# Following a short TensorE matmul with a long one from another thread, and new step times in the scheduler's recorded clock

## The chip, the core and the metric

The kernel runs on one core of a Trainium2 chip. The metric is the device time of one execution, in microseconds (us). The profile names the engines PE (TensorE matmuls), PEld (TensorE weight loads), DVE (VectorE), ACT (ScalarE), POOL (GpSimd) and SP (SyncE, which starts the transfers).

## The reference

Two layers of a diffusion backbone work on 256 context tokens and 512 latent tokens of width 1024. Cut to what matters:

```
u = rms_norm(h) * (1 + scale) + shift                 # scale, shift, gate = silu(c) @ w_ada
rq, rk, rv, rg, gq, gk, gv, gg, glr, ma, mb = split(u @ w_in)
ret = chunked retention of rq, rk, rv, both directions, 4 heads
gla = chunked gated linear attention of gq, gk, gv, decay from glr, both directions, 4 heads
y_ret = (group_norm(ret) * silu(rg)) @ w_branch_ret
y_gla = (head_rms_norm(gla) * silu(gg)) @ w_branch_gla
h = h + gate * ((sigmoid(ma) * y_ret + sigmoid(mb) * y_gla) @ w_out)
```

After the second layer the latent stream gets a last rms_norm. The second layer needs no outputs for the context tokens.

## The kernel before, in words

Every large product is made as three products of rounded parts (`mm3`: high by high, high by low, low by high), accumulated in PSUM. A matmul instruction has a 128x128 stationary operand, loaded by its own weight load, and a moving operand whose columns decide its length: 512 for projections over the latent tokens or over a weight block (into `pj` tiles), 256 for projections over the context, for the states (`xp`), for the outputs of a head (`op`) and for the branch projections that read the normalised heads `z`, and 128 for score products and for transposes (`tr`, line 319, into `xp`). The program holds 10,136 matmul instructions: 3,104 of 512 columns, 192 of 384, 5,968 of 256, 848 of 128 and 24 of 2. Below, "short" means under 256 columns and "long" the others.

The order on every engine comes from a scheduler that runs while the kernel is built (class `Emit`). Work is written as threads, generators that record instructions. They are ranked: evacuations of PSUM, weights, scans (the heads' transposes, scores, states, outputs), low, and main (the projections). The scheduler holds a recorded clock for each engine. `run` goes through the threads in rank; an instruction for another engine than PE is issued once it is ready on the recorded clock, and of the PE instructions that are ready, the first in rank is issued. The recorded clocks settle only the order: the chip waits on semaphores, so a wrong estimate makes an engine wait, or puts work later than need be.

The cost of a matmul on the recorded clock is set in `mm` and `tr`, and the clock is moved on in `issue`:

```
c = (max(n, 256) if r.dtype == F32R else max(4 * n, 512)) / 2400 + 0.0023
...
self.op("pe", 0.11, (i,), (o,), lambda: self.nc.tensor.transpose(o, i, ident))
```

That is 0.216 us for 512 columns, 0.109 us for 256 and for 128, and 0.11 us for a transpose.

Of the kernel before, what the change touches and what calls it, by code (L numbers as in the profile page):

```python
# [13 lines left out]
F32R = mybir.dt.float32r  # L14
# [29 lines left out]
def _pieces():  # L44
    """Name of every 4 KiB-per-partition weight piece of a layer, in the order of use."""
    names = []
    for h in range(H):
        names += [("rqkv", h, i) for i in range(4)] + [("rg", h, j) for j in range(2)]
    for oc in range(KC):
        names += [("ma", oc), ("wr", oc)]  # L50
    names.append(("glr",))
    for h in range(H):
        names += [("gk", h), ("gq", h)] + [("gv", h, i) for i in range(2)] + [("gg", h, j) for j in range(2)]
    for oc in range(KC):
        names += [("mb", oc), ("wg", oc)]
    names += [("wo", oc) for oc in range(KC)]
    return {n: i for i, n in enumerate(names)}
# [125 lines left out]
def view(ap, off, dims):  # L183
    """A free-form view of a tile: its partitions, and [step, count] pairs from element off on."""
    return bass.AP(tensor=ap.tensor, offset=ap.offset + off, ap=[list(ap.ap[0])] + [list(d) for d in dims])
# [11 lines left out]
EVAC, WEIGHTS, SCAN, LOW, MAIN = range(5)  # L197

# [20 lines left out]
class Emit:  # L219
    """Puts the program into order. The work is written as threads: generators that record instructions and name, at  # L220
    each yield, what they need to go on. Whenever an engine is about to run dry, the first thread in rank whose next
    instruction there has its operands is let through. The clocks are estimates that settle nothing but this order."""

    def __init__(self, nc, sb, ps, dr):
        self.nc, self.sb, self.ps, self.dr = nc, sb, ps, dr
        self.uid = 0
        self.clk = {"pe": 0.0, "act": 0.0, "dve": 0.0, "pool": 0.0, "sp": 0.0, "dma": 0.0}
        self.end = {}
        self.table = None
        self.free_n = dict(SLOTS)  # L230
        self.slot = {k: [0.0] * n for k, n in SLOTS.items()}
        self.threads = []
        self.cur = None
        self.subs = []
        self.began = set()
        self.read = {}
        self.tick, self.cols, self.warm = 0, 0, False

    # tiles
# [45 lines left out]
    # instructions  # L285
# [3 lines left out]
    @staticmethod  # L289
    def keys(aps):  # L290
        """What instructions wait on: tiles, or the token groups of a stream tile."""
        r = []
        for a in aps:
            if isinstance(a, bass.AP):
                nm = a.tensor.name
                if nm.startswith("stream"):
                    t = a.offset % T
                    r += [(nm, g) for g in range(t // 256, (t + a.shape[-1] - 1) // 256 + 1)]
                else:
                    r.append(nm)  # L300
        return tuple(r)
# [5 lines left out]
    def mm(self, o, l, r, start, stop):  # L307
        n = self.n(r)
        c = (max(n, 256) if r.dtype == F32R else max(4 * n, 512)) / 2400 + 0.0023
        self.op("pe", c, (l, r), (o,), lambda: self.nc.tensor.matmul(o, l, r, start=start, stop=stop))  # L310
        self.cur.queue[-1].cols = n if r.dtype == F32R else 4 * n
# [6 lines left out]
    def tr(self, o, i, ident):  # L318
        self.op("pe", 0.11, (i,), (o,), lambda: self.nc.tensor.transpose(o, i, ident))  # L319
# [41 lines left out]
    def split_to(self, x, tag="g"):  # L361
        """The parts of x in new tiles: (hi, lo)."""
        shape = x.shape[1:]
        h, l = self.get(tag, shape, F32R), self.get(tag, shape, F32R)
        self.split(h[0], l[0], x)
        return h, l
# [8 lines left out]
    # order  # L375
# [7 lines left out]
    def after(self, gen, prio=SCAN, heavy=False):  # L383
        """Spawns a thread when all that its maker has recorded is out."""
        self.pseudo(lambda: self.spawn(gen, prio, heavy))

    def fill(self, th):
        """Lets a thread record its next step, if it has all it asked for."""
# [5 lines left out]
        for tag in SLOTS:  # L394
            n = w.get(tag, 0)
# [15 lines left out]
    def issue(self, th, op, ready):  # L411
        th.queue.pop(0)
        e = op.eng
        t = max(self.clk[e], ready)
# [5 lines left out]
        else:  # L420
# [4 lines left out]
            if e == "pe":  # L425
                c *= self.pace(t, op.cols)
# [11 lines left out]
    def lag(a, b):  # L438
        """From the end of one engine's instruction to the start of another's that waits for it."""
# [4 lines left out]
    def pace(self, t, cols):  # L444
        """TensorE's clock rests in a tick after one with few columns."""
# [7 lines left out]
    def run(self):  # L453
        while self.threads:
            now = self.clk["pe"]
            soon, moved, first = None, False, None
            for th in list(self.threads):
# [27 lines left out]
                if ok <= now and e == "pe":  # L485
                    first = first or (th, op, ready)
                elif ok <= now:
# [5 lines left out]
            if not moved and first:  # L493
                self.issue(*first)
# [5 lines left out]
class Weights:  # L500
    """The weight pieces in the order of their use, loaded and split ahead of it."""
# [44 lines left out]
class Block:  # L546
    """A weight block of 8 chunks of the contraction, n columns wide, taken half a piece at a time."""
# [24 lines left out]
def body(ctx, tc, io, out):  # L572
# [11 lines left out]
    # ---- constants  # L584
# [20 lines left out]
    # ---- the order of the projections, and with it that of the weights  # L605
# [30 lines left out]
    # ---- norm over the model width  # L636
    class Norm:
# [5 lines left out]
        def add(self, g, kp, h):  # L643
            """A step of a thread: h holds two chunks of a group's stream [128, 2, 256]."""
# [61 lines left out]
    # ---- conditioning  # L706
# [17 lines left out]
    def load_c():  # L724
        """silu(c) of both streams along the free axis, on all partitions: four tiles (vector, half)."""
# [16 lines left out]
    def ada_dve(cr, junk, raw, acc):  # L742
        """acc [128, 2, 2] (vector, half) = the rows of a transposed piece times both conditioning vectors."""
# [14 lines left out]
    def ada_first(kp, C, A, ev, begun):  # L758
        """Conditioning of two chunks in the first layer: the shift on VectorE, the scale on TensorE."""
# [37 lines left out]
    def ada_late(todo, done, then=None):  # L797
        """Conditioning that is not needed yet, on VectorE."""
# [32 lines left out]
    # ---- pieces shared by the two branches  # L831
# [14 lines left out]
    def spawn_states(hd, full):  # L846
        """The two state recurrences of a head. hd.kd[g]: hi, lo [128 tok, dir, tile, dk]."""
# [38 lines left out]
    def out_tile(hd, o, i, t, ph, pl, qh, ql):  # L886
        """o [128 tok, dv] of one tile: the scores' part and what the states bring."""
# [12 lines left out]
    def gate_out(hd, on, gain, g):  # L900
        """Normalised heads [tok, 2, dv] times gain and gate, feature-major."""
# [46 lines left out]
    def feat(src, sp, evac, wait=None):  # L948
        """Feature-major products with a weight block; src(k, a, n) gives parts of [a, a + n) as (offset, hi, lo)."""
# [22 lines left out]
    # ---- retention  # L972
# [91 lines left out]
    def rproj_outer(l, hd, R, full, u_ev, begun):  # L1064
        """The first head's projection, chunk by chunk of the contraction as the chunks come."""
# [131 lines left out]
    # ---- gated linear attention  # L1197
# [48 lines left out]
    def gdec(hd, Z):  # L1246
        """hd.G[g] [channel, dir, token]: the decay logs summed within each 128 tokens (times 16)."""
# [172 lines left out]
    # ---- merge  # L1420
    def gate_pair(B, pair, full, late):
        """The merge gates of two output chunks."""
# [80 lines left out]
    def out_unit(l, gs, hold, norm, m_ev, read_ev, hk, hn):  # L1503
        """The output projection of some groups, the gated residual, and the squares for the next norm."""
# [28 lines left out]
    def last(kp, g, h, norm):  # L1533
        """The final norm's gain and the output."""
# [5 lines left out]
    # ---- the whole  # L1540
# [137 lines left out]
```

## Time and profile before

| | |
|---|---|
| time, median of 3 runs | 1609.39 us (1609.18 to 1609.75) |
| span of the profiled execution (the page gives no other time of it) | 1609.0 us |
| PE busy | 1582.4 us (98%) |
| PEld busy | 1438.7 us (89%) |
| DVE busy | 1110.1 us (69%) |
| ACT busy | 837.7 us (52%) |

The span runs from the first to the last instruction of the one profiled execution. Busy time of PE overlaps: a matmul's recorded duration is longer than the distance to the next one's start, so the distance between starts is what counts. Chains of waits, rows of the timeline and waits by engine are in the section of rows.

### The profile page before, as it was taken

How to read it: one execution, taken by the hardware profiler on the slowest of the kernel's cores; microseconds unless marked ns; L12 is line 12 of the kernel's file. 1: busy time of each engine (PE TensorE's matmuls, PEld its weight loads, DVE VectorE, ACT ScalarE, POOL GpSimd, SP SyncE). 2: the span in 40 equal slices, each digit the busy share in tenths (PEclk: the TensorE clock that was granted, in tenths of full speed). 3: DMA queues.
4: the chain of work that ended last, by engine and by line, in shares of the span. 5: the costliest groups of instructions: out<-in, count | busy, mean ns of one | idle time of the engine just before them, and what ended most of it. 6: DMA issues, size and time to landing. Idle time of an engine off the chain costs nothing.

```text
span 1609.0 us, 26505 instructions
## 1 busy us (share of the span) xinstructions
PE 1582.4 (98%) x10224; PEld 1438.7 (89%) x10224; DVE 1110.1 (69%) x2526; ACT 837.7 (52%) x1783; POOL 37.7 (2%) x52
## 2 busy tenths in 40 slices
PE   7999999999999999999999999999999999999997
PEld 4788888989998999998998988988899999898997
DVE  8877485617877868776396765776657778877465
ACT  6734143421267778666333653443424767857443
POOL 0000000000000000000000000000000000000000
PEclk9999999999999999999999999999999999999999
DMA  9312122216621112112356421321355211213452
GB/s 347 128 46 66 45 67 66 92 54 236 209 67 53 60 47 66 42 53 91 128 200 205 146 71 58 92 79 53 118 199 170 65 66 53 80 54 103 155 186 92
DMA packets 71182, 169.37 MB, mean 105 GB/s; under 512 B 7440, under 2 KB 15760, under 8 KB 71056
## 3 DMA queue, kind: packets, MB, share of 16 engines
q1 hardware_dynamic: 71056, 167.69, 31.6%
q8 instruction: 80, 1.31, 0.3%
q14 instruction: 46, 0.38, 0.1%
HBM read 151.93 MB, written 15.73 MB: 104 GB/s over the span
## 4 chain that ended last, share of the span: by engine, by line
PE 93%; DVE 2%; issue 2%; ACT 1%; DMA 1%; POOL 0%; SPq 0%; POOLq 0%; DVEq 0%; ACTq 0%
PE pj L310 78%; PE xp L310 8%; PE op L310 6%; PE xp L319 2%; ACT g L329 1%; DVE g L342 0%; DVE p L342 0%; DVE g L352 0%; POOL v L370 0%; ACT p L329 0%; DMA g<-in_xT 0%; DMA wraw<-in_w 0%; DVE wlo L342 0%; SPq L373 0%; ACT whi L329 0%
## 5 line engine op out<-in xcount | busy, mean ns | idle before, releaser
L310 PE MATMUL pj<-streamh,whi 128*128 128x512 f32 (+1 forms) x1280 | 441.9, 346 | 0.6 <-ACT g L329 0.6
L310 PE MATMUL pj<-streaml,whi 128*128 128x512 f32 (+1 forms) x1280 | 441.4, 345 | 0.6 <-DVE streaml L342 0.6
L310 PE MATMUL pj<-streamh,wlo 128*128 128x512 f32 (+1 forms) x1248 | 430.5, 345 | 0.0
L329 ACT ACTIVATE whi<-wraw 128x512 fp32r<-128x512 f32 x350 | 217.5, 629 | 271.9 <-PE pj L310 248.4
L342 DVE TENSOR_TENSOR wlo<-wraw,whi 128x512 fp32r<-128x512 f32 x350 | 236.7, 686 | 161.8 <-ACT whi L329 159.8
L310 PEld LDWEIGHTS pj<-streamh,whi 128*128 128x128 f32 x1280 | 242.8, 190 | 26.1 <-ACT g L329 1.0
L310 PEld LDWEIGHTS pj<-streaml,whi 128*128 128x128 f32 x1280 | 242.9, 190 | 24.3 <-DVE streaml L342 0.8
L329 ACT ACTIVATE g<-g 128x512 fp32r<-128x512 f32 (+2 forms) x428 | 227.9, 564 | 64.9 <-DVE g L352 30.4
L310 PEld LDWEIGHTS pj<-streamh,wlo 128*128 128x128 f32 x1248 | 236.6, 190 | 24.3
L310 PE MATMUL pj<-whi,streamh 128*128 128x256 f32 (+2 forms) x744 | 247.8, 333 | 0.8 <-ACT whi L329 0.6
L310 PE MATMUL pj<-wlo,streamh 128*128 128x256 f32 (+2 forms) x744 | 247.8, 333 | 0.3 <-DVE wlo L342 0.3
L310 PE MATMUL pj<-whi,streaml 128*128 128x256 f32 (+2 forms) x744 | 247.3, 332 | 0.3 <-DVE streaml L342 0.3
L329 ACT ACTIVATE g<-pj 128x256 f32<-128x256 f32 (+4 forms) x296 | 107.6, 397 | 241.7 <-PE pj L310 241.3
L310 PE MATMUL pj<-g,whi 128*128 128x256 f32 x1280 | 230.5, 283 | 0.0
L342 DVE TENSOR_TENSOR g<-g,g 128x512 fp32r<-128x512 f32 (+2 forms) x312 | 198.2, 649 | 32.1 <-ACT g L329 30.1
L310 PEld LDWEIGHTS pj<-g,whi 128*128 128x128 f32 x1280 | 199.9, 192 | 0.3
L310 PE MATMUL pj<-g,wlo 128*128 128x256 f32 x640 | 181.1, 283 | 0.0
L310 PE MATMUL xp<-g,g 128*128 128x256 f32 (+1 forms) x928 | 152.2, 277 | 2.1 <-DVE g L342 1.8
L310 PEld LDWEIGHTS pj<-whi,streamh 128*128 128x128 f32 x744 | 141.5, 190 | 12.7 <-ACT whi L329 0.7
L310 PEld LDWEIGHTS pj<-whi,streaml 128*128 128x128 f32 x744 | 141.6, 190 | 11.8 <-DVE streaml L342 0.7
L310 PEld LDWEIGHTS pj<-wlo,streamh 128*128 128x128 f32 x744 | 141.5, 190 | 11.9 <-DVE wlo L342 0.5
L342 DVE TENSOR_TENSOR g<-pj,g 128x128 f32<-128x128 f32 (+4 forms) x163 | 60.9, 410 | 128.3 <-ACT g L329 128.2
(99 smaller groups left out, 1832.7 us busy)
## 6 DMA issues: line engine op xcount, KB each, us to landing
wraw<-in_w SPq DMA_DIRECT2D x175, 512.0 KB, 3.6
g<-in_adat SPq DMA_DIRECT2D x80, 256.0 KB, 4.7
g<-in_w SPq DMA_DIRECT2D x38, 256.0 KB, 5.5
g<-in_xT SPq DMA_DIRECT2D x24, 256.0 KB, 5.2
z<-g SPq DMA_DIRECT2D x20, 256.0 KB, 2.0
g<-z SPq DMA_DIRECT2D x20, 256.0 KB, 4.2
m<-g SPq DMA_DIRECT2D x20, 256.0 KB, 3.4
g<-m SPq DMA_DIRECT2D x20, 256.0 KB, 4.8
```

Of the source, the lines that this page charges most:

```text
L310: self.op("pe", c, (l, r), (o,), lambda: self.nc.tensor.matmul(o, l, r, start=start, stop=stop))
L319: self.op("pe", 0.11, (i,), (o,), lambda: self.nc.tensor.transpose(o, i, ident))
L329: lambda: self.nc.scalar.activation(out=out, in_=in_, func=func, scale=scale, **kw), TABLE.get(func))
L342: lambda: self.nc.vector.tensor_tensor(out=out, in0=a, in1=b, op=op))
```

## The change

Two things change in the scheduler, and nothing in what is computed. First, `issue` remembers whether the last PE instruction was short. If it was, `run` issues the first ready PE instruction in rank that is long, where there is one, and not the first in rank. Second, the recorded clock gets other step times: 0.0133 us are added to the columns' time instead of 0.0023, a short one costs at least 0.06 us and no longer 0.109, and a weight load takes 0.108 us and may start when the matmul before it starts. Comments and docstrings also go, which moves line numbers by 3 to 8.

```diff
+STEP, LOAD, SHORT = 0.0133, 0.108, 0.06
...
+        self.mm_at = self.ld_at = -1.0
+        self.short = False
...
     def mm(self, o, l, r, start, stop):
         n = self.n(r)
-        c = (max(n, 256) if r.dtype == F32R else max(4 * n, 512)) / 2400 + 0.0023
+        c = max(n / 2400 + STEP, SHORT) if r.dtype == F32R else max(4 * n / 2400 + 0.005, 2 * LOAD)
...
     def tr(self, o, i, ident):
-        self.op("pe", 0.11, (i,), (o,), lambda: self.nc.tensor.transpose(o, i, ident))
+        self.op("pe", SHORT, (i,), (o,), lambda: self.nc.tensor.transpose(o, i, ident))
...
             if e == "pe":
+                ld = max(self.mm_at, self.ld_at + LOAD)
+                t = max(t, ld + SHORT)
+                self.mm_at, self.ld_at, self.short = t, ld, op.cols < 256
                 c *= self.pace(t, op.cols)
...
                 if ok <= now and e == "pe":
                     first = first or (th, op, ready)
+                    if op.cols >= 256:
+                        long = long or (th, op, ready)
...
             if not moved and first:
-                self.issue(*first)
+                self.issue(*(long if long and self.short else first))
```

The two places below are on PE. A row has the line, the instruction, the tile written, the tiles read and the output's size.

The first is in the second layer's retention, where four transposes of a head's queries and values come due (`cst` is the identity) beside state products (`xp<-g,g`) and a projection (`pj`). Before:

```order
L310 MATMUL xp_10928<-g_10709,g_10923 128x256
L310 MATMUL xp_10930<-g_10710,g_10922 128x256
L310 MATMUL xp_10930<-g_10709,g_10923 128x256
L319 MATMUL xp_10932<-cst,g_10805 128x128 x4
L310 MATMUL pj_10872<-whi_10680,streamh_84 128x512
L310 MATMUL xp_10943<-g_10709,g_10922 128x256
L310 MATMUL xp_10943<-g_10710,g_10922 128x256
```

With the change:

```order
L322 MATMUL xp_10932<-cst,g_10798 128x128
L313 MATMUL pj_10872<-whi_10678,streamh_84 128x512
L322 MATMUL xp_10932<-cst,g_10798 128x128
L313 MATMUL xp_10942<-g_10701,g_10922 128x256
L313 MATMUL xp_10942<-g_10702,g_10922 128x256
L313 MATMUL xp_10942<-g_10701,g_10923 128x256
L313 MATMUL xp_10949<-g_10701,g_10922 128x256
L313 MATMUL xp_10949<-g_10702,g_10922 128x256
L313 MATMUL xp_10949<-g_10701,g_10923 128x256
L322 MATMUL xp_10932<-cst,g_10798 128x128
L313 MATMUL pj_10872<-wlo_10679,streamh_84 128x512
L322 MATMUL xp_10932<-cst,g_10798 128x128
```

The four transposes stood in one run, and now each has long matmuls behind it. In the whole program the short ones stood in 196 runs, 38 of them of a single matmul and 78 of four; now they stand in 837 runs, 827 of them single. Of the singles 25 were followed by a matmul of 256 columns and 13 by one of 512 before; now 420 are followed by 256, 389 by 512 and 18 by 384. In 325 of the stretches between two shorts there is now exactly one matmul of 256 columns, and in 300 exactly one of 512.

The second place is at the end of the second layer's last gated head: its last four transposes, and the branch projection that reads the head's `z`. Before, the transposes were followed by 24 matmuls of 512 columns of the merge gates and then by the branch projection, of which the first rows with `z` of the last group (`g_17134` high, `g_17135` low) are shown:

```order
L310 MATMUL pj_17197<-g_16980,whi_16907 128x256
L310 MATMUL pj_17197<-g_16981,whi_16907 128x256
L310 MATMUL pj_17197<-g_16980,wlo_16908 128x256
L310 MATMUL pj_17197<-g_17134,whi_16907 128x256
L310 MATMUL pj_17197<-g_17135,whi_16907 128x256
L310 MATMUL pj_17197<-g_17134,wlo_16908 128x256
```

With the change (`xp_17211` are the transposes, `g_17213` and `g_17214` the high and low part of the `z` made of them):

```order
L322 MATMUL xp_17211<-cst,g_17201 128x128
L313 MATMUL pj_17154<-g_16386,whi_16889 128x256
L322 MATMUL xp_17211<-cst,g_17201 128x128
L313 MATMUL pj_17154<-g_16385,wlo_16890 128x256
L322 MATMUL xp_17211<-cst,g_17201 128x128
L313 MATMUL pj_17154<-g_16445,whi_16889 128x256
L313 MATMUL pj_17154<-g_16446,whi_16889 128x256
L313 MATMUL pj_17154<-g_16445,wlo_16890 128x256
L313 MATMUL pj_17154<-g_17013,whi_16889 128x256
L313 MATMUL pj_17154<-g_17014,whi_16889 128x256
L313 MATMUL pj_17154<-g_17013,wlo_16890 128x256
L313 MATMUL pj_17154<-g_17213,whi_16889 128x256
```

The first use of the last `z` stood 63 long matmuls behind the last transpose, and now stands six behind it.

## Rows read from the trace of the kernel before

**Rows 1.** The page: span, and the chain that ended last by engine.

```profile
span 1609.0 us, 26505 instructions
...
PE 93%; DVE 2%; issue 2%; ACT 1%; DMA 1%; POOL 0%; SPq 0%; POOLq 0%; DVEq 0%; ACTq 0%
```

**Rows 2.** Busy time by stretch: length, engines, granted clock, DMA share, GB/s.

```profile
0.00:35.00 35.00, 23.52 (x112) 16.07 (x113) 27.12 (x78) 20.52 (x38) 2.75 (x7) 0.90 0.98 344
35.00:495.00 460.00, 459.42 (x2857) 410.82 (x2856) 310.58 (x807) 187.04 (x400) 9.44 (x12) 1.00 0.31 101
495.00:735.00 240.00, 236.95 (x1660) 220.03 (x1659) 177.66 (x337) 182.24 (x406) 8.72 (x10) 1.00 0.16 52
...
925.00:930.00 5.00, 3.90 (x22) 3.13 (x20) 4.54 (x12) 3.61 (x6) 0.00 (x0) 0.99 0.62 200
...
1275.00:1500.00 225.00, 224.60 (x1462) 204.19 (x1461) 174.59 (x327) 163.08 (x364) 6.17 (x8) 1.00 0.22 71
```

**Rows 3.** Waits of PE: us in total, times, longest.

```profile
PE pj L310 <- DMA cst<-in_cst: 4.7, 1, 4.7
...
PE op L310 <- ACT g L329: 0.5, 1, 0.5
```

**Rows 4.** Timeline, PE: a single short between matmuls of 256 columns.

```profile
522.01 0.28 PE L310 MATMUL pj<-whi,streamh 128*128 128x256 f32 x1
...
524.05 0.22 PE L310 MATMUL xp<-g,g 128*128 128x128 f32 x1
524.11 0.34 PE L310 MATMUL pj<-whi,streaml 128*128 128x256 f32 x1
524.29 0.28 PE L310 MATMUL pj<-whi,streamh 128*128 128x256 f32 x1
...
524.52 0.28 PE L310 MATMUL pj<-whi,streaml 128*128 128x256 f32 x1
```

**Rows 5.** Timeline, PEld: the weight loads at the same place.

```profile
524.05 0.19 PEld L310 LDWEIGHTS pj<-whi,streaml 128*128 128x128 f32 x1
...
524.16 0.19 PEld L310 LDWEIGHTS pj<-whi,streamh 128*128 128x128 f32 x1
```

**Rows 6.** Timeline, PE: a single short between matmuls of 512 columns.

```profile
506.93 0.39 PE L310 MATMUL pj<-streamh,wlo 128*128 128x512 f32 x1
...
508.29 0.22 PE L310 MATMUL xp<-g 128*128 128x128 f32 x1
...
508.63 0.39 PE L310 MATMUL pj<-streamh,whi 128*128 128x512 f32 x1
...
509.10 0.33 PE L310 MATMUL xp<-g,g 128*128 128x128 f32 x2
```

**Rows 7.** Timeline, PE: a run of four shorts before matmuls of 512 columns.

```profile
1143.10 0.60 PE L319 MATMUL xp<-cst,g 128*128 128x128 f32 x4
...
1143.77 0.39 PE L310 MATMUL pj<-streamh,whi 128*128 128x512 f32 x1
...
1144.92 0.39 PE L310 MATMUL pj<-streamh,wlo 128*128 128x512 f32 x1
```

**Rows 8.** Timeline, PE: a run of four shorts before matmuls of 256 columns.

```profile
540.15 0.60 PE L319 MATMUL xp<-cst,g 128*128 128x128 f32 x4
540.50 0.48 PE L310 MATMUL op<-g,p 128*128 128x256 f32 x2
540.82 0.64 PE L310 MATMUL op<-g,g 128*128 128x256 f32 x4
```

**Rows 9.** Timeline of three engines: last transposes of the last gated head, to `z`.

```profile
1497.99 0.80 PE L319 MATMUL xp<-cst,g 128*128 128x128 f32 x4 [0.40 <-ACT g L329]
...
1498.83 0.48 DVE L352 SCALAR_TENSOR_TENSOR g<-xp,small,g 128x256 f32<-128x256 f32 x1 [1.95 <-PE xp L319]
...
1500.34 0.63 ACT L329 ACTIVATE g<-g 128x512 fp32r<-128x512 f32 x1 [0.98 <-DVE g L352]
...
1501.01 0.69 DVE L342 TENSOR_TENSOR g<-g,g 128x512 fp32r<-128x512 f32 x1 [0.70 <-ACT g L329]
```

More of the change, by code (lines that the diff above doesn't have):

```diff
@@ L455, in run @@
             now = self.clk["pe"]
-            soon, moved, first = None, False, None
+            soon, moved, first, long = None, False, None, None
             for th in list(self.threads):
```

## The prediction

> **What bounds the kernel now.** I read the page first: of a span of 1609.0 us the chain that ended last is TensorE's for 93% [rows 1]. [...] The first 35 us, with 11.5 us idle, wait for transfers and the first norm, and the diff changes nothing they consist of. The products of a head's outputs, which read the states, waited for ACT once, 0.5 us [rows 3]. So two sums decide: what the sequence of matmuls costs when nothing waits, and the few microseconds of waits.
>
> Next, what one matmul costs in that sequence: the timeline, read by the distance between starts, since recorded durations overlap. Seventeen matmuls of 256 columns start within 522.01 to 524.05, so 0.120 us each; six of 512 within 506.93 to 508.29, so 0.227 us each [rows 4, 6].
>
> **The change: its first part, a long matmul behind a short.** It pays if a short followed by a long costs less than one followed by a short. The price of a short is read as the time from its start to the start of the second matmul behind the run, less one long step.
>
> Run of four before 256: 540.15 to 540.82 holds four shorts and two longs (the row of x2), 0.67 - 2 x 0.120 = 0.43, or 0.108 each; the trace has 30 such runs [rows 8]. Run of four before 512: 1143.10 to 1143.77 is 0.67 - 0.227 = 0.443, or 0.111 each; 29 such runs [rows 7].
>
> Single between 256s: it starts at 524.05, the long behind it only 0.06 later, which looks like a bargain. But the next long starts at 524.29, 0.18 after the one before it and not 0.12. The short has cost 0.24 - 0.12 = 0.12; over the 24 places of this kind the median is 0.116 [rows 4]. Between 512s: 508.29 to 508.63 is 0.34 - 0.227 = 0.115 with the starts unrounded, the median of ten places [rows 6]. The reason stands in the load rows: the weight load for the matmul behind the short starts with the short, at 524.05, and the load after that at 524.16. A load holds its place for 0.11 us, the short has columns for about half of that, and the remainder is waited for, whoever comes next [rows 5]. The early start of the long is a recorded start; the time comes back in its own step.
>
> So a single is dearer than a member of a run. The order holds 789 more singles than before: 395 with 256 columns behind, 376 with 512, 18 with 384.
> - Behind 256: 0.116 - 0.109 (the median of the 30 runs) = 0.007, x 395 = 2.8 us. Bounds: at 524.29 to 524.52 two steps take 0.23 and not 0.24, so some of it comes back; at 0.003 it is 1.2 us, and at the rounded 0.12 - 0.112 it is 3.2.
> - Behind 512: 0.115 - 0.111 = 0.004, x 376 = 1.5 us. Bounds: the two steps behind the single take 508.63 to 509.10, 0.47 and not 0.454, so it may cost 0.131 in all, while the five steps behind the run of four take 1.15 and not 1.135, so a member costs 0.115: a difference of 0.016, 6.0 us at most; at least 0, if the after-effect does not repeat when shorts and longs alternate strictly, of which the trace has no stretch.
> - Behind 384: 18 x 0.006 = 0.1 us.
>
> Sum: **+4.4 us**, with bounds from +1.2 to +9.3.
>
> [...]
>
> **The second part, the recorded clock.** No instruction is added. For 512 columns the recorded step goes from 0.216 to 0.227, for 256 from 0.109 to 0.120, which are the steps of the trace [rows 4, 6]. A short went in at 0.109 or 0.11, near its real 0.11; now it moves the clock by 0.067, or 0.108 behind another short, so a single is some 0.02 to 0.05 too cheap. The recorded clock of longs ran 5 to 10% ahead of the chip and the slack this left goes. A chain of 1.6 us on DVE and ACT was covered by 1.6 / 0.109 = 14.7 matmuls of 256 columns, which take 1.76 us, and is now covered by 13.3, 1.60 us: 0.17 us less. Where more than that was to spare nothing is felt, and that the output products waited only 0.5 us in all says it mostly was [rows 3]. I set this at 0, with bounds: all 5.1 us of idle time behind 35 us gone, or 24 of the chains (four heads, two branches, three groups) late by 0.17 us, 4 us.
>
> **One place where the order itself makes a wait.** In the second layer's last gated head the last transposes now stand six matmuls ahead of the first use of their `z`, where 63 stood before. The chain was seen there before [rows 9]: the row of four transposes ends at 1498.79, and with the 0.22 or more that one lasts [rows 4] the last starts at about 1498.5; DVE's first product starts at 1498.83 and the second can follow after some 0.40, since only a weight's split stood between; it lasts 0.48 and ends at 1499.71. ACT's high part starts 0.03 behind (1500.34 against 1499.83 + 0.48) and takes 0.63, to 1500.37: 1.87 behind the start of the last transpose. The cover is 0.116 for the transpose and 6 x 0.120, 0.84. The high part is late by 1.0 us. The low part, DVE's 0.69 with 0.04 ahead of it, comes 0.73 later for a matmul due 0.12 later, so 0.6 more. Together **+1.6 us**, behind which all of main's branch projection stands in PE's queue. Bounds: 0, if work ahead of it waits in its place (main has then got ahead), and 2.2, if 0.3 us of semaphores lie in each of two hops as in some rows' idle times. The 24 merge-gate matmuls that were the cover come earlier; their work is the same.
>
> Order on SP moves with the recorded clock, but transfers take 0.16 to 0.62 of the queues' time behind 35 us, and PE's one wait for a transfer, 4.7 us, is the one at the start [rows 2, 3]; I take 0.
>
> **Sum.** 1609.0 + 4.4 + 0 + 1.6 = 1615.0 us of span; the median of the runs lies 0.4 above the profiled span, so 1615.4 us.
>
> **Rivals.**
> - *The change does what it says.* If the early start of the long were real, a single would cost 0.06 (the distance of starts [rows 4]) and not 0.11: 789 x 0.05 = 39 us less, about 1572 us. For it speaks that step alone; against it the next step, 0.18, in all 24 places. [...] Chance 0.06.
> - *Nothing measurable.* Singles at their lower bound, +1.2, with the late `z` offset by waits that a truer clock avoids in the first layer's gated heads (3.05 us idle in 495 to 735 [rows 2]): 1609.4 + 1.2 + 1.6 - 3 = 1609.2; anything to 1612.6 counts here. Chance 0.24.
> - *Faster through the clock alone.* Longs at true steps place the dependent shorts where operands land, and all 5.1 us of idle time go, with singles at their lower bound and no late `z`: 1609.4 + 1.2 - 5.1 = 1605.5. It decides once the waits fall by 4.4 more than the singles cost. Against it: the 5.1 contain the boundary between the layers, 1.10, a chain that no order shortens. Chance 0.07.
> - *Dearer than forecast.* Slack was thinner than the one short wait suggests and the 160 state steps each lose the 0.17 us: 27 us at worst, half of it 14, about 1629 us. Against it: that one wait [rows 3]. Chance 0.06.
>
> **How the numbers follow.** The forecast, slower by some 6 us, has 0.57, with its own range 1612.6 to 1622 (upper bounds 9.3 + 2.2 + about 1). The likeliest time is 1615.4. The range 1606.5 to 1622.5 takes in the forecast, the case of nothing measurable and a little of the faster one, 0.83. A measurement of this kernel can tell about 0.2%, 3.2 us, from no change. Faster: 0.06 + 0.07 = 0.13. Same: 0.24. Slower: 0.57 + 0.06 = 0.63.
>
> **What the profile after would show.** Singles with a recorded step of 0.06 and a long behind them of 0.17 to 0.18 (256) or 0.285 (512), where the forecast holds; steps of 0.12 and 0.227 behind them, where the first rival does. In strict alternation a pair of short and 512 should take 0.342 to 0.36 us and one with 256 0.233 to 0.24. A wait of about 1.0 us, then one of 0.6, of a `pj` matmul for ACT and DVE near 1490 to 1510 us. The clock stays at 1.00. I would be wrong if the pairs are shorter than a run's sum, or if waits of PE between 35 and 1600 us change by more than 4 us either way.

## The result, and the profile after

The changed kernel takes 1625.20 us (median of 4 runs, 1623.65 to 1627.75) against 1609.34 us before (1609.18 to 1609.75): ratio 1.0098, 95% interval 1.0084 to 1.0113. It is slower by 15.9 us. The forecast had the sign, 1615.4 us and a range to 1622.5, so the time lies outside. The profiled execution took 1627.75 us with a span of 1626.0; the other three have spans of 1624.0, 1621.9 and 1622.8, and mean granted clocks of 0.993, 0.995 and 0.994 against its 0.991.

The page of the kernel after, with the lines that answer to [rows 1] (span, then PE's busy time, the granted clock in 40 slices, and the chain that ended last by engine):

```profile
span 1626.0 us, 26498 instructions
...
PE 1596.8 (98%) x10224; PEld 1437.3 (88%) x10224; DVE 1113.7 (68%) x2526; ACT 836.8 (51%) x1780; POOL 35.6 (2%) x52
...
PEclk8999999999999999999999999999999999999998
...
PE 90%; DVE 4%; ACT 2%; issue 2%; DMA 1%; POOL 0%; SPq 0%; POOLq 0%; DVEq 0%; ACTq 0%
```

PE looks as busy as before, 98%; the row of digits hides what happened. The chain tells a little more: DVE's share goes from 2 to 4% and ACT's from 1 to 2%, at PE's expense. The stretches show where (columns as in [rows 2]):

```profile
0.00:35.00 35.00, 25.00 (x105) 16.23 (x105) 25.81 (x75) 19.81 (x37) 3.14 (x7) 0.80 0.98 349
35.00:495.00 460.00, 460.00 (x2839) 406.86 (x2839) 310.18 (x806) 187.16 (x397) 8.55 (x12) 1.00 0.30 99
495.00:735.00 240.00, 237.94 (x1669) 220.40 (x1667) 178.92 (x338) 175.21 (x398) 8.01 (x10) 1.00 0.17 54
945.00:1150.00 205.00, 203.74 (x1101) 176.16 (x1100) 138.85 (x357) 84.52 (x190) 5.51 (x8) 1.00 0.24 75
1275.00:1400.00 125.00, 122.61 (x815) 110.85 (x813) 95.88 (x181) 92.10 (x199) 2.76 (x4) 0.99 0.20 64
1390.00:1395.00 5.00, 3.98 (x14) 3.29 (x15) 4.43 (x9) 2.64 (x5) 0.00 (x0) 0.66 0.30 27
1500.00:1530.00 30.00, 27.93 (x170) 25.12 (x170) 14.14 (x27) 15.26 (x35) 0.69 (x1) 0.94 0.25 87
1520.00:1530.00 10.00, 8.33 (x55) 7.92 (x54) 4.61 (x10) 2.81 (x6) 0.00 (x0) 0.83 0.17 54
```

Between 1275 and 1400, where before PE had hardly an idle moment [rows 2], it now idles 2.4 us, and at 1390 to 1395 its granted clock is 0.66. From 1500 to 1530 it idles 2.1 us, with 0.83 in the last ten. The first 35 us have 0.80 where they had 0.90. The first layer's gated heads (495 to 735) idle less than before, 2.06 against 3.05.

Waits of PE in the kernel after (us in total, times, longest), to be held against [rows 3]:

```profile
PE xp L322 <- DVE g L345: 2.0, 1, 2.0
PE xp L313 <- DVE g L345: 1.6, 2, 1.4
PE pj L313 <- ACT g L332: 1.3, 1, 1.3
PE xp L313 <- DVE g L355: 1.3, 4, 0.3
...
PE pj L313 <- DVE g L345: 0.3, 1, 0.3
```

The first is at 1389, the second mostly at 680, the fourth are four state products of the second layer's retention, and the third and the last are the late `z` of the last gated head.

**An account by starts.** Busy time hides losses, because a matmul's record runs into the next one. So I took the distance from each start on PE to the next and subtracted the plain steps: 0.120, 0.174 and 0.227 us for a matmul of 256, 384 and 512 columns, 0.110 for a short. The excess is put to half clock where the granted clock in the trace stood at its lower level, 0.5; the traces of the kernels before and after hold no value but 1.0 and 0.5. Else it is put to a wait where it is over 0.15 us and the matmul began within 0.3 us of the end of the DVE, ACT or POOL instruction whose semaphore it waited for. The rest is put to singles (a short alone, and the long behind it) or to runs and other matmuls. Where waits end and dear steps begin depends on such bounds: with 0.1 in place of 0.15, the waits of a kernel come out 0.1 to 1.2 us higher. In us:

| kernel | waits, 35 to 1595 | half clock, 35 to 1595 | singles | runs and others | first 35 us |
|---|---|---|---|---|---|
| before | 7.7 | 1.4 | 0.2 | 8.0 | 16.8 |
| after | 14.8 | 2.9 | 4.2 | 11.0 | 17.9 |

The differences add up to 16.7 of the 17.0 us between the spans: 7.1 us are waits, 1.5 half clock, 7.0 (4.0 and 3.0) dearer steps with nothing waiting, 1.1 the start. The rest lies ahead of the first matmul and behind 1595 us.

**The wait at 1389.** The timeline of PE in the kernel after (start, duration, what; idle time and its releaser in brackets):

```profile
1386.59 0.40 PE L313 MATMUL pj<-streamh,whi 128*128 128x512 f32 x1
1386.83 0.28 PE L322 MATMUL xp<-cst,g 128*128 128x128 f32 x1
1386.86 0.47 PE L313 MATMUL pj<-streaml,whi 128*128 128x512 f32 x1
1387.17 0.27 PE L322 MATMUL xp<-cst,g 128*128 128x128 f32 x1
...
1388.66 0.40 PE L313 MATMUL pj<-streaml,whi 128*128 128x512 f32 x1
1391.02 0.30 PE L322 MATMUL xp<-cst,g 128*128 128x128 f32 x1 [1.96 <-DVE g L345]
...
1392.93 0.63 PE L313 MATMUL pj<-streaml,whi 128*128 128x512 f32 x1
1393.36 0.63 PE L313 MATMUL pj<-streamh,wlo 128*128 128x512 f32 x1
...
1394.92 0.39 PE L313 MATMUL pj<-streamh,whi 128*128 128x512 f32 x1
1395.15 0.39 PE L313 MATMUL pj<-streaml,whi 128*128 128x512 f32 x1
```

The alternation at the top is the new rule: from short to short 1386.83 to 1387.17, 0.34 us, so the short costs 0.34 - 0.227 = 0.11 and not 0.03, as its recorded start would have it. Then the transposes of the decayed keys stand first in PE's queue for an operand that isn't there. DVE shows why; it had itself waited 1.38 us for ACT. Its queue there:

```profile
1386.92 0.69 DVE L350 TENSOR_SCALAR g<-xp 128x512 f32<-128x512 f32 x1
1388.99 0.69 DVE L350 TENSOR_SCALAR g<-xp 128x512 f32<-128x512 f32 x1 [1.38 <-ACT g L332]
1389.60 0.68 DVE L345 TENSOR_TENSOR g<-pj,g 128x512 fp32r<-128x512 f32 x1
1390.19 0.68 DVE L345 TENSOR_TENSOR g<-g,g 128x512 f32<-128x512 f32 x1
```

The last of three DVE instructions in series ends at 1390.87, and the transposes start 0.15 later. In the kernel before the same transposes of that layer had 0.23 to 0.64 us to spare in all twelve places; the closest, DVE and then PE:

```profile
1390.63 0.67 DVE L342 TENSOR_TENSOR g<-g,g 128x512 f32<-128x512 f32 x1
...
1391.52 0.60 PE L319 MATMUL xp<-cst,g 128*128 128x128 f32 x4
```

From the end at 1391.30 to the start at 1391.52 is 0.22: no wait, but hardly cover either. The wait in the kernel after isn't all that it costs: behind it the steps of 512 columns are 0.43 us (1392.93 to 1393.36), until at 1394.92 they are 0.23 again. There the granted clock is 0.5, from 1391.34 to 1394.75 us, which begins 0.3 us after the end of this wait of 2.1 us; it costs 1.47 us more.

**The late `z`**, in the kernel after, on PE, DVE and ACT:

```profile
1520.48 0.27 PE L322 MATMUL xp<-cst,g 128*128 128x128 f32 x1
...
1520.60 0.69 DVE L345 TENSOR_TENSOR wlo<-wraw,whi 128x512 fp32r<-128x512 f32 x1 [2.19 <-ACT whi L332]
...
1521.18 0.28 PE L313 MATMUL pj<-g,wlo 128*128 128x256 f32 x1
...
1521.20 0.87 DVE L355 SCALAR_TENSOR_TENSOR g<-xp,small,g 128x256 f32<-128x256 f32 x2
1522.11 0.63 ACT L332 ACTIVATE g<-g 128x512 fp32r<-128x512 f32 x1 [1.54 <-DVE g L355]
...
1522.79 0.39 PE L313 MATMUL pj<-g,whi 128*128 128x256 f32 x1 [1.33 <-ACT g L332]
...
1523.52 0.39 PE L313 MATMUL pj<-g,whi 128*128 128x256 f32 x1 [0.34 <-DVE g L345]
...
1524.66 0.63 PE L313 MATMUL pj<-g,whi 128*128 128x256 f32 x2
...
1525.09 0.41 PE L313 MATMUL pj<-g,wlo 128*128 128x256 f32 x1
```

It is where the forecast put it. The high part is late by 1.49 us (1.61 from the start before it to 1522.79, less a step of 0.12) and the low part by 0.61 (0.73 less 0.12). Forecast were 1.0 and 0.6. Of the half microsecond more, 0.4 is the weight split on DVE at 1520.60: it stands ahead of both products with `xp`, which start only at 1521.20, while the forecast had one product ahead of it. Behind the two waits the granted clock is 0.5 again, from 1524.46 to 1527.87 us (two steps take 0.43 us from 1524.66 to 1525.09, where one takes 0.12 at a granted clock of 1.00), for 1.41 us more than its steps.

### The profile page after: what moved, and what is told of

Its sections match the earlier page's. It is cut to its first block, busy times and chain, and to the rows that moved or that the text cites. A ratio compares the mean times of both kernels' runs of the same rounds, so it can differ in the third digit from the quotient of the medians.

```text
span 1626.0 us, 26498 instructions
## 1 busy us (share of the span) xinstructions
PE 1596.8 (98%) x10224; PEld 1437.3 (88%) x10224; DVE 1113.7 (68%) x2526; ACT 836.8 (51%) x1780; POOL 35.6 (2%) x52
## 4 chain that ended last, share of the span: by engine, by line
PE 90%; DVE 4%; ACT 2%; issue 2%; DMA 1%; POOL 0%; SPq 0%; POOLq 0%; DVEq 0%; ACTq 0%
PE pj L313 75%; PE xp L313 7%; PE op L313 5%; PE xp L322 2%; DVE g L345 2%; ACT g L332 1%; DVE wlo L345 1%; DMA g<-in_xT 1%; DMA wraw<-in_w 1%; DVE g L355 1%; ACT p L332 0%; ACT whi L332 0%; POOL v L373 0%; DVE p L345 0%; DVE streaml L345 0%
## 5 line engine op out<-in xcount | busy, mean ns | idle before, releaser
L313 PE MATMUL pj<-streaml,whi 128*128 128x512 f32 (+1 forms) x1280 | 451.3, 353 | 0.6 <-DVE streaml L345 0.6
L313 PE MATMUL pj<-streamh,whi 128*128 128x512 f32 (+1 forms) x1280 | 450.1, 352 | 0.0
L313 PE MATMUL pj<-streamh,wlo 128*128 128x512 f32 (+1 forms) x1248 | 440.0, 353 | 0.0
L332 ACT ACTIVATE g<-g 128x512 f32<-128x512 f32 (+2 forms) x428 | 230.4, 565 | 82.2 <-DVE g L345 38.2
L313 PE MATMUL pj<-whi,streamh 128*128 128x256 f32 (+2 forms) x744 | 251.4, 338 | 1.6 <-ACT whi L332 1.1
L313 PE MATMUL pj<-wlo,streamh 128*128 128x256 f32 (+2 forms) x744 | 252.3, 339 | 0.0
L313 PE MATMUL pj<-whi,streaml 128*128 128x256 f32 (+2 forms) x744 | 251.8, 338 | 0.0
L313 PE MATMUL xp<-g,g 128*128 128x256 f32 (+1 forms) x928 | 185.4, 261 | 3.0 <-DVE g L345 1.6
L313 PEld LDWEIGHTS xp<-g,g 128*128 128x128 f32 x928 | 157.7, 190 | 16.2 <-DVE g L345 3.0
```

Source lines behind the costliest of these rows:

```text
L332: lambda: self.nc.scalar.activation(out=out, in_=in_, func=func, scale=scale, **kw), TABLE.get(func))
```

## The experiments

Every kernel was run beside the kernel before on the same chip; the intervals are 95%. The account by starts of all of them stands in a table at the end of this section.

### First: the two parts alone, and the price of a short

**e1_rule** has the new rule on the old recorded clock. Its edit, in `run`, against the kernel before:

```diff
-            self.issue(*first)
+            self.issue(*(long if long and self.short else first))
```

> The rule alone (a short matmul is followed by a long one where one is ready), with the recorded clock of before. 823 single shorts in the order. Theory A (singles cost some 4 us of stream as forecast, and the rest of the loss, waits and the lower clock behind them, comes from the new step times): 1613 to 1616 us, +4 to +6, and the cold stretch at the start as short as before. Theory B (all the loss comes from the rule, which draws out the dependent chains by putting a long matmul between their shorts; the step times are harmless): 1620 to 1626 us, with the waits of the changed kernel.

Measured: 1620.57 us (1619.32 to 1622.04) against 1609.48, ratio 1.0069 (1.0054 to 1.0084). The rule alone costs 11 us, with 823 singles; that is theory B's range.

**e2_clock** has the new recorded clock and not the rule. Its edit, against the kernel after:

```diff
-                self.issue(*(long if long and self.short else first))
+                self.issue(*first)
```

> The new step times alone, with the first ready instruction in rank issued as before. 35 single shorts. Theory A: no stream cost, but the added waits and cold stretches: 1617 to 1621 us. Theory B: 1608 to 1611 us.

Measured: 1629.73 us (1627.79 to 1630.76), ratio 1.0122 (1.0105 to 1.0139). The clock alone, which the forecast set at 0, costs 20 us, with hardly a single short in its order. It is the dearer part.

**e3_price** is the kernel after with a recorded 0.111 us for a short, transposes too, and no recorded loads; **e4_true** is the same without the rule.

```diff
-        c = max(n / 2400 + STEP, SHORT) if r.dtype == F32R else max(4 * n / 2400 + 0.005, 2 * LOAD)
+        c = max(n / 2400 + STEP, 0.111) if r.dtype == F32R else max(4 * n / 2400 + 0.005, 2 * LOAD)
...
-                ld = max(self.mm_at, self.ld_at + LOAD)
-                t = max(t, ld + SHORT)
```

> The rule, and a recorded clock in which a short costs the 0.111 us that the trace shows, whatever stands around it; longs at the new steps; no weight loads in the clock. 824 single shorts. Theory A: stream +4, waits less than half of the changed kernel's since the clock no longer runs ahead at every single: 1613 to 1619 us. Theory B: as the changed kernel, 1622 to 1627 us.

> The recorded clock of the run before (a short at 0.111 us, longs at the new steps) without the rule. 44 single shorts. Theory A: no stream cost; what the lost slack of the longs costs by itself shows here: 1609 to 1614 us. Theory B: 1608 to 1611 us.

Measured: e3 1627.82 us (1627.09 to 1628.56), ratio 1.0114 (1.0099 to 1.0129); e4 1634.05 us (1632.86 to 1635.56), ratio 1.0153 (1.0138 to 1.0168). A recorded clock whose steps are all as on the chip makes the worst order of the four. With either of the new clocks the rule wins something back: 1629.73 to 1625.20 with the change's prices, 1634.05 to 1627.82 with the true ones. The two parts do not add: 11 + 20 is 31, and together they cost 16. The times of e2, e3 and e4 lie above every range named for them, e4's by 20 us.

### Second: does the order of shorts cost anything in itself

**e5_stream** takes the kernel's work away and sends PE blocks of matmuls that wait for nothing, 60 of each kind, first with 512 columns for the long ones, then with 256.

```diff
-    e.spawn(main(), MAIN)
+        for long in (512, 256):
+            for block in ([long] * 8, [128] * 4 + [long] * 4, [128, long] * 4, [128] * 8):
+                for _ in range(60):
+                    for n in block:
+                        e.mm(o[k % 2][0][:, :n], h[0][:, k % 4 * P:k % 4 * P + P], h[0][:, :n], True, True)
+                        k += 1
```

> Leaves out the whole of the reference: PE runs streams of matmuls that wait for nothing, sixty times each block: eight of 512 columns; four shorts, then four of 512; short and 512 in turn, four times; eight shorts; and the same four with 256. Theory A (a single costs some nanoseconds more than a member of a run, whatever comes behind): a block of run and four 512s takes 1.35 us, the alternating one 1.37 to 1.40; with 256 columns 0.915 and 0.93 to 0.95; a short in eight 0.108 to 0.112. The rule's own theory (a single costs 0.06): alternating blocks of 1.15 and 0.72 us.

Stretches inside six of its sections: runs of four before 512, the alternation with 512, shorts alone, 256 alone, runs of four before 256, the alternation with 256 (columns: length, then busy and count of PE, PEld, ACT, POOL, granted clock, DMA share, GB/s):

```profile
120.00:190.00 70.00, 70.00 (x411) 61.36 (x410) 0.00 (x0) 0.00 (x0) 1.00 0.00 1
200.00:270.00 70.00, 70.00 (x413) 61.59 (x412) 0.00 (x0) 0.00 (x0) 1.00 0.00 1
280.00:330.00 50.00, 50.00 (x450) 50.00 (x449) 0.00 (x0) 0.00 (x0) 1.00 0.01 1
340.00:380.00 40.00, 40.00 (x336) 40.00 (x335) 0.00 (x0) 0.00 (x0) 1.00 0.00 1
400.00:440.00 40.00, 40.00 (x351) 40.00 (x350) 0.00 (x0) 0.00 (x0) 1.00 0.01 1
450.00:495.00 45.00, 45.00 (x391) 45.00 (x390) 0.00 (x0) 0.00 (x0) 1.00 0.00 1
```

The same 70 us hold 411 matmuls in runs and 413 in alternation. From the sections' first and last starts, over 60 blocks each: a block of 8 x 512 takes 1.847 us with a step of 0.227 inside, four shorts and four of 512 take 1.3667 in a run and 1.3601 alternating; four shorts and four of 256 take 0.9200 and 0.9257; eight shorts 0.892. Less the long steps of 0.227 (443 matmuls in 100 us of the first section, 0.226 each) and 0.120 a short is 0.115 in a run and 0.113 alternating beside 512, 0.110 and 0.111 beside 256, 0.1115 among its like. So the order of shorts is worth 2 ns one way and 1 ns the other. The early start of the long behind a short is given back at once, which ends the rival in which the change does what it says. But the forecast's extra price of a single isn't here either. In the kernel after the median single is 0.117 with a long of 512 behind it (383 places) and 0.111 with one of 256 (413): the 4 ns at 512 belong to something that the stream lacks.

### Third: too little cover?

The forecast's own bound for the recorded clock was cover: longer recorded steps put fewer matmuls between a producer and its consumer. **e7_f103** and **e10_f95** scale the recorded cost of every matmul, transposes too, in the kernel before, by 1.03 and 0.95. The line of e7:

```diff
-        c = (max(n, 256) if r.dtype == F32R else max(4 * n, 512)) / 2400 + 0.0023
+        c = 1.03 * ((max(n, 256) if r.dtype == F32R else max(4 * n, 512)) / 2400 + 0.0023)
```

> The kernel before, with all recorded matmul costs 3% higher and nothing else; longs are then still 2 to 6% cheaper than on the chip. Theory C: waits grow with the cover lost, about a third of the way to the run with the true clock: 1614 to 1619 us. If the cover is not what counts but what the shorts cost in the clock: 1608 to 1611 us.

> The kernel before with all recorded matmul costs 5% lower, so that the recorded clock runs still further ahead of the chip and each chain gets more cover. Theory C (cover decides the waits): PE's waits between 35 and 1590 us, 7.4 us before, halve: 1603 to 1608 us. Theory D (the order before happens to suit this set of numbers, and any other set gives more waits): 1611 to 1618 us.

Measured: e7 1616.83 us (1616.27 to 1617.98) against 1609.88, ratio 1.0043 (1.0028 to 1.0058); e10 1610.19 us (10 runs, 1609.08 to 1612.17) against 1609.75, ratio 1.0004 (0.9994 to 1.0013). Three per cent more on the recorded clock cost 7 us; five per cent less bring nothing.

The waits of PE from 495 to 735 us, the first layer's gated heads, tell how that goes: transposes of a head's outputs that wait for ACT. The kernel before, then e10, e7, e2 and e4:

```profile
PE xp L319 <- ACT g L329: 0.9, 2, 0.6
```

```profile
PE xp L319 <- ACT g L329: 0.6, 2, 0.4
```

```profile
PE xp L319 <- ACT g L329: 3.1, 7, 0.7
```

```profile
PE xp L322 <- ACT g L332: 3.7, 7, 0.7
```

```profile
PE xp L322 <- ACT g L332: 4.3, 8, 0.7
...
PE xp L313 <- ACT g L332: 0.3, 1, 0.3
```

All waits of this stretch by the account, with the recorded step of a long of 256 columns beside them: e10 0.104 us, 2.1; before 0.109, 4.0; e7 0.113, 5.9; e2 0.120 with cheap shorts, 8.6; e4 0.120 with shorts at 0.111, 9.5. In five kernels without the rule the waits rise with the recorded step, as they would if cover decided them.

It can be seen in the operands that are not late, too. For every matmul of states, scores, outputs, transposes and branch products that waits on a semaphore of ACT or DVE between 35 and 1595 us, I took the time from the end of the instruction whose semaphore count it waits for to the matmul's start. Where PE stood idle for the operand this time was 0.05 to 0.15 us (1522.79 and 1391.02 above), so that a matmul under 0.2 had nothing to spare. Under 0.2 us, and under 0.5, are:

| kernel | under 0.2 us | under 0.5 us | of |
|---|---|---|---|
| e10_f95 | 25 | 65 | 627 |
| before | 25 | 125 | 650 |
| e7_f103 | 74 | 233 | 643 |
| e2_clock | 102 | 279 | 619 |
| e4_true | 128 | 329 | 631 |
| e1_rule | 26 | 113 | 629 |
| after | 79 | 201 | 621 |
| e11_lagb | 32 | 74 | 647 |
| e6_lag40 | 83 | 178 | 625 |

The rule changes the margins little (before to e1, 125 to 113 under 0.5 us). The recorded clock takes them away.

e10 wins 1.9 us in the stretch and loses most of it at 65.8 us, where a projection waits 1.7 us for ACT's rounded stream, for an operand that before was in time.

**e11_lagb** gives the kernel before more cover in another way: the time from a producer's recorded end to PE's start goes from 0.25 to 0.40 us. **e6_lag40** does the same in the kernel after.

```diff
-        return 0.25 if b == "pe" else 0.2 if a == "pe" else 0.14
+        return 0.4 if b == "pe" else 0.2 if a == "pe" else 0.14
```

> The kernel before with 0.40 us in place of 0.25 recorded between another engine's instruction and the matmul that waits for it. Theory C: 1604 to 1608 us. Theory D: 1611 to 1620 us.

> The changed kernel, with 0.40 us in place of 0.25 recorded between another engine's instruction and the matmul that waits for it, so that each chain gets back about the cover that the longer recorded steps took. Theory C (the waits come from the cover lost with the true steps of the longs): PE's waits between 35 and 1590 us fall from 12 us to under 5, time 1613 to 1619 us. Theory B (the waits come from the rule's order): as the changed kernel, 1623 to 1627 us.

Measured: e11 1615.45 us (6 runs, 1614.62 to 1617.32) against 1609.75, ratio 1.0034 (1.0021 to 1.0046); e6 1631.25 us (1630.31 to 1632.12) against 1609.88, ratio 1.0134 (1.0117 to 1.0151). Both are slower than the kernels they start from. In e6 the waits from 495 to 735 fall a little, from 3.1 to 2.6 us; in e11 they rise, from 4.0 to 6.8. In e11 the lag does what it should to most margins, 74 under 0.5 us against 125. But the few that are late are later: two groups of transposes stand idle 2.1 us for DVE in that stretch, one of them 1.4, and five 2.1 us for ACT. So more cover on the whole does not mean fewer microseconds of waits. Theory C missed in all three runs that were to give cover back (e10, e11, e6), and e11 fell into the range of theory D: the order before suits its set of numbers, and most others give more waits. The runs show that longer recorded steps thin the margins and add waits; they do not show that cover alone decides the time.

### Fourth: the late `z`, and the rule only in places

**e9_early** is the kernel after with the rule off in the last part of the program (from 1440 us of the recorded clock), so that the last transposes stand in a run again, 40 matmuls ahead of their `z`.

```diff
-                self.issue(*(long if long and self.short else first))
+                self.issue(*(long if long and self.short and now < 1440 else first))
```

> The changed kernel with the rule off once the recorded clock is past 1440 us, which is the end of the second layer's gated heads; 801 singles stay. The last transposes then stand in one run, 40 matmuls ahead of the first use of their z. If the late z costs what the changed kernel's trace shows there (waits of 1.5 and 0.6 us and 1.4 us at half clock behind them): 3 to 4 us under the changed kernel, 1621 to 1622.5 us. If the time comes back later: as the changed kernel, 1624 to 1626 us.

**e12_rulemid** is e1 with the rule off in the first projection and from the second layer's last merge gates on; **e13_lagmid** has the same rule, the change's clock and the lag of 0.40.

```diff
+                self.issue(*(long if long and self.short and self.rule else first))
...
+                e.rule = u != ("rproj", 0) and not (l == DEPTH - 1 and kind in ("mb", "wg", "out"))
```

> The rule alone with the recorded clock of before, but off in the first head's projection (the start) and from the second layer's last merge gates on, so that the late z and the longer start go; 772 singles stay. If singles are free in the stream, as the streams without waits showed, and the rule alone lost by those two places: 1610 to 1613 us. If the rule draws out chains everywhere: 1616 to 1620 us, hardly less than the rule alone.

> The changed kernel with the 0.40 us of recorded lag, and the rule off at the same two places. The run with the lag alone had 3 us less of waits up to 1500 us than the changed kernel, and lost them behind; if both hold here: 1614 to 1619 us. If the lag only moves waits about: 1621 to 1626 us.

Measured: e9 1622.56 us (1622.42 to 1623.36) against 1609.88, ratio 1.0079 (1.0064 to 1.0094), just above the 1621 to 1622.5 named for the late `z`; e12 1613.91 us (7 runs, 1613.55 to 1615.43) against 1609.75, ratio 1.0026 (1.0015 to 1.0037), between its two ranges; e13 1617.35 us (1616.93 to 1618.56), ratio 1.0048 (1.0033 to 1.0062), in its first range. (What was said ahead of e13, that e6 waits less than the kernel after up to 1500 us, the account does not bear out: 12.1 against 11.4 us.) The stretch 1500 to 1530 in e6, e9 and e12:

```profile
1500.00:1530.00 30.00, 24.21 (x138) 21.23 (x137) 12.41 (x23) 14.80 (x31) 0.69 (x1) 0.89 0.21 70
```

```profile
1500.00:1530.00 30.00, 29.37 (x200) 26.85 (x200) 14.45 (x29) 15.11 (x34) 1.06 (x1) 1.00 0.34 108
```

```profile
1500.00:1530.00 30.00, 29.67 (x227) 28.25 (x226) 12.84 (x26) 13.19 (x26) 0.69 (x1) 1.00 0.49 166
```

With the rule off there, PE idles 0.6 and 0.3 us instead of 2.1 and its granted clock is 1.00. The excess of this stretch falls from 4.4 us in the kernel after to 1.1 in e9, and from 5.8 in e1 to 0.8 in e12. Where the rule stays on, the scheduler itself runs dry at this place: PE's recorded clock stands still for 2.0 us in the kernel after, 3.8 in e1, 2.3 in e3 and 6.4 in e6 (excess on the chip 4.4, 5.8, 2.3 and 9.6), and not at all in e9, e12 and e13. So the rule is the cause at this place. How it does it is argued and not shown by itself: most long ones that it brings forward are main's, the last in rank; main so gets ahead of the scans until only the last head's chain is left, and then every hop of it is waited for.

The account by starts for all of them, in us, 35 to 1595 where nothing else is said:

| kernel | waits | half clock | singles | runs and others | first 35 us | excess, 1500 to 1530 |
|---|---|---|---|---|---|---|
| e1_rule | 12.6 | 1.5 | 3.5 | 9.7 | 18.1 | 5.8 |
| e2_clock | 18.2 | 3.8 | 0.6 | 13.1 | 17.5 | 0.8 |
| e3_price | 16.7 | 0.0 | 5.2 | 11.6 | 16.9 | 2.3 |
| e4_true | 21.2 | 2.9 | 1.0 | 15.3 | 16.7 | 0.6 |
| e6_lag40 | 19.1 | 2.9 | 4.2 | 10.1 | 16.4 | 9.6 |
| e7_f103 | 12.3 | 0.0 | 0.2 | 10.0 | 16.9 | 0.2 |
| e9_early | 12.4 | 0.7 | 3.8 | 10.8 | 17.4 | 1.1 |
| e10_f95 | 7.9 | 0.0 | 0.2 | 8.3 | 15.9 | 0.2 |
| e11_lagb | 11.9 | 1.5 | 0.3 | 9.4 | 17.2 | 0.5 |
| e12_rulemid | 8.7 | 0.0 | 3.4 | 8.3 | 17.3 | 0.8 |
| e13_lagmid | 10.4 | 0.0 | 3.7 | 9.2 | 16.6 | 0.7 |

e12 shows the price of singles nearly by itself: its waits (8.7) are 0.4 us under the waits and half clock of the kernel before (9.1), and still its span is 4.0 us longer, of which dearer steps make 3.5 (3.4 + 8.3 against 0.2 + 8.0) and the start 0.5. No version here is faster than the kernel before.

## Why the prediction was wrong

**Singles, +4.4 (bounds 1.2 to 9.3): near, in part by luck.** Steps with nothing waiting cost 7.0 us more in the kernel after, 5.0 in e1 and 3.5 in e12. That is within the bounds. The step-by-step reading, by the second start behind a short, was right: alternating pairs take 0.344 and 0.232 us, where 0.342 to 0.36 and 0.233 to 0.24 were named. Of the 7.0 us, 4.0 are the singles themselves; the other 3.0 lie at runs and other matmuls and are not explained. That the 4.0 come so near to 4.4 is luck: the median single with 256 columns behind it is 0.111 where the forecast had 0.116, and with 512 it is 0.117 where it had 0.115, so one part was priced too high and the other too low. Nor is it shown why a single before 512 costs 4 ns more here than in e5; there the shorts are plain products that all read one tile, here most are transposes and scores beside busy engines.

**The recorded clock, 0 (bounds -5.1 to +4): the step that failed.** "I set this at 0" rested on one row, an output product that waited 0.5 us [rows 3], from which I read that more than the 0.17 us taken away "mostly was" to spare. The row was misread. Its one wait is no product of a head's outputs, but a small one of the conditioning in the first 35 us, which writes into an `op` tile too:

```profile
25.83 0.60 PE L310 MATMUL op<-cst,g 2*128 2x2 f32 x4 [0.51 <-ACT g L329]
```

So output products did not wait at all, while state products and transposes did: the first layer's gated heads held 4.0 of the 7.7 us of waits before. e2 prices the part at 20 us. In the kernel after the waits outside the late `z` are 5.0 us more (14.8 - 7.7 - 2.1), of which e1, with the rule on the old clock, has 1.3. A row of waits says which chains were late; it can't say how near to late the others were. The margins can: 125 of 650 were under 0.5 us, of which 0.05 to 0.15 passed even where PE stood idle for the operand, and with the longer recorded steps of the kernel after 201 of 621 are. They could have been read from the trace of before. e7 and e10 show the same from outside: the order before stands just on the flat side. Five per cent faster on the recorded clock brings nothing, three per cent slower costs 7 us. Of the bounds, the 5.1 us are the idle time of PE behind 35 us in [rows 2], 0.58 + 3.05 + 1.10 + 0.40, and the 4 us failed too: they priced 24 chains with one hop each, and in e4 the waits come to 21.2 us, 13.5 more than before, in 43 places where before had 12. The forecast had named a change of PE's waits by more than 4 us as a sign that it is wrong: by starts they change by 7.1.

**The late `z`, +1.6 (bounds 0 to 2.2): right place, 1.9 us too small.** Waits of 1.49 and 0.61 us and 1.41 at half clock make 3.5. (The transposes' own 0.55 us for ACT at 1519 were there before [rows 9].) I had costed the chain and left out a split in DVE's queue and what PE does after a wait. The 0.3 us of semaphores in each hop that the bound of 2.2 takes do not show there: the hops took 0.04 us from DVE to ACT (1522.07 to 1522.11), 0.05 from ACT to PE (1522.74 to 1522.79) and 0.06 from DVE to PE (1523.46 to 1523.52).

**"The clock stays at 1.00": wrong.** It fell to 0.5 behind the wait at 1389 and behind the late `z`, for 3.4 us each time and at a cost of 1.47 and 1.41 us, where the kernel before had one such place, 929.9 us, at the boundary of the layers. Four runs of the same program differ by 4.1 us of span and by their mean clocks in the same order, so part of the 16 us is not a fixed sum. e3 bears that out: it has the same late `z`, with waits of 1.43 and 0.61 us from 1523 to 1525, and the granted clock stays at 1.00:

```profile
1520.00:1530.00 10.00, 8.38 (x67) 7.84 (x67) 4.68 (x11) 3.42 (x7) 0.69 (x1) 1.00 0.18 54
```

**The first 35 us, "the diff changes nothing they consist of": nearly.** Their excess is 17.9 against 16.8 us, at a granted clock of 0.80 against 0.90 [rows 2]. But e1, e2 and e7 with other orders have 16.9 to 18.1, so this may be the moment at which the clock rises from 0.5 to 1.00 (22.0 us before, 26.0 after) and not the order; that is left open.

**The sum of the miss.** 2.6 (steps) + 5.0 (waits) + 1.9 (late `z` with its half clock) + 1.1 (start) + 0.1 (other half clock) is 10.7, between the forecast's 6.0 and the account's 16.7. The largest term is the waits that were put at 0.

**The rivals.** The first is dead by e5. "Dearer than forecast", given a chance of 0.06, came nearest: its mechanism, thin slack, is what e2, e4 and e7 show. Its size was too large: against its 14 us and 27 at worst, the kernel after has 5.0 us of such waits, e2 10.5 more than before and e4 13.5. "Faster through the clock alone" had the sign wrong; true steps made the worst order (e4).

**What stays open.** Why a few waits grow long in e11 while most margins widen; why the rule wins back 4.5 to 6 us once the clock is changed (e2 to after, e4 to e3); and how much of the waits comes from cover and how much from leaving an order that happened to fit. A greedy order in rank answers a shift of 0.15 us by other neighbours for everything behind it, which fits all three but is argued, not shown.

## What to carry to other kernels

A scheduler's estimated times are part of its tuning: an estimate that is 5% too fast may be what keeps consumers far enough behind their producers, and making it true takes that away. Before pricing such a change by the waits that are there, ask how far each chain is from waiting, which the margins from producer's end to consumer's start tell in the trace, or one run with the estimates scaled a few per cent up and one down. And where an engine's queue gets a new first in line, charge the wait, what the clock may lose behind it (1.47 and 1.41 us here, nothing in e3), and whatever else the producer's queue holds ahead of the operand (0.4 us of a weight split here).

## What the runs showed of the hardware

- In e5 a short matmul costs 0.110 to 0.115 us in each kind of company, though in the kernel before the matmul behind a single starts only 0.06 us later by the record (524.05 to 524.11 [rows 4]). Around that single, weight loads start 0.11 us apart [rows 5], so the step fits that of its own load; no order run here hid it.
- In the kernel after the granted clock went to 0.5 for 3.4 us twice: 0.3 us after the wait of 2.1 us, and 0.9 us after two waits of 1.5 and 0.6 us in a row. In e3 the same two waits cost no clock (1.00 from 1520 to 1530 us), and 16.7 us of waits between 35 and 1595 us, the longest 1.8, none either. Why the clock fell in one case and not in the other is left open.
